# Feed-forward units of a Hymba-style layer: a unit's stores issued one product later, and the splits of the new operands at the turn spread over other products

## The chip, the cores and the metric

The kernel runs on one core of one Trainium2 chip. The metric is the device time of one execution in microseconds (us). Every kernel is run several times, and its time is the median of the runs.

## What is computed

One layer of a bidirectional encoder, in float32, on a sequence of 2048 rows of 1024 values: a modulated RMSNorm, one input projection, windowed attention beside a two-way mLSTM, one output projection with a gated residual, and then a feed-forward part with its own modulated norm and gated residual. The change lies in the feed-forward part alone, which in the reference is

```
h = rms_norm(x, g_norm2) * (1 + scale) + shift        # 2048 x 1024
gu = h @ w_ffn_in                                     # 1024 x 5632
g, u = split(gu, 2)                                   # D_FF = 2816 columns each
x = x + gate * ((silu(g) * u) @ w_ffn_out)            # 2816 x 1024
```

## The kernel before

**A matrix product in three.** TensorE multiplies float32 operands that are split into a high part (`hi`, rounded by a copy on ScalarE) and the rest (`lo`, a subtraction on VectorE). One product of float32 precision is three matmuls, hi by hi, hi by lo and lo by hi (function `mm3`, L56 to L58).

**Seven products for eight.** Both feed-forward matrix products go by a Strassen scheme (Winograd's form): a 2 by 2 block product by seven block products instead of eight. The seven row operands, in the order of use B11, B21, T2, T1, T3, B22 and T4, are sums and differences of blocks of `h`. They lie in DRAM in `hop_d` and are split into resident tiles in SBUF, two tiles of hi and two of lo for each operand. The seven weight operands of a unit (A11, A12, S2, S1, S3, S4, A22) are made from the raw weights by Pool and split by ScalarE and VectorE while the unit before runs (function `weights`, L1455 to L1467).

**A unit.** Function `pair` is one unit: the products 0 to 6, each of 12 matmuls (four times `mm3`), and between them the work on their sums. Three PSUM banks are used, `ps1` for the products 0, 2, 4 and 6, `ps2` for product 1, and `ps5` for products 3 and 5; product after product is added up in the same bank. So a product must wait for the copy of what the bank held before it: product 2 for `s` (L1613, after product 0), product 4 for `u` (L1619), product 5 for `c` (L1624, after product 3), product 6 for `u` (L1627, after product 4). All of these are on ScalarE. There too stands the tanh `t` (L1620), which waits for VectorE's `g` (L1616, the sum of product 1 and `s`), and it stands ahead of `c`. Later in the unit VectorE does `u` (L1631) and `u` (L1633), with the tanh `t` (L1632) on ScalarE between them, and after product 6 L1640. Pool does L1628 and L1639, in the units of one half of the columns L1645, and at the end of each pair of units L1654, L1656 and L1658. The results of a unit go to DRAM (`a_d`); they are put on the list `late`, and the next unit issues their stores on SyncE (function `stores`, L1590).

**The row of units.** There are 44 units: the first 22 on one half of the rows, the other 22 on the other half. The unit in which the first half is used for the last time (number 21, counted from 0) is called the turn. While it runs, the seven operands of the other half are brought in, in the tiles that its products leave: `start(u)` after product `u` loads operand `u` (two DMAs of 512 KB on SyncE, L1412), and `finish(u)` splits it, two copies on ScalarE (L1416) and two subtractions on VectorE (L1417). At the turn `finish` takes operands 0, 1, 2, 3 and 4 after the products 1, 2, 3, 4 and 6; the operands 5 and 6 are split in unit 22, after its products 0 and 1. No weights are prepared during the turn; unit 22 uses weights that are there already, and prepares those of unit 23 from its product 2 on (STEPS).

**What sets the order.** Every engine works through its instructions in the order in which the code writes them. `beside(u)`, called as `then(u)` between two products, writes the splits at the turn and the making of weights into that order. Engines wait for each other by semaphores alone.

The tile names in the rows of the profile are these: `fp` is a PSUM bank of a unit, `B` and `T` are row operands, `A` and `S` are weight operands, and `sf`, `graw` and `A22r` are raw weights and their sums.

Of the kernel before, what the change touches and what calls it, by code (L numbers as in the profile page):

```python
# [36 lines left out]
def hybrid_layer_kernel(  # L37
# [14 lines left out]
    def bank(tag, name):  # L52
        return pp.tile([P, 512], F32, tag=tag, name=name, bufs={"g": 2, "a": 2, "b": 1, "c": 2, "d": 1}[tag])

    def mm3(o, lh, ll, rh, rl, first, last, skip=False):
        pe.matmul(o, lh, rh, start=first, stop=False, skip_group_check=skip)  # L56
        pe.matmul(o, lh, rl, start=False, stop=False, skip_group_check=skip)  # L57
        pe.matmul(o, ll, rh, start=False, stop=last, skip_group_check=skip)  # L58
# [218 lines left out]
    s1 = xs.enter_context(tc.tile_pool(name="sx", bufs=2, side="left", reuse_waits="tile"))  # L277
# [881 lines left out]
    for s_ in range(len(order) + 2):  # L1159
# [22 lines left out]
        u2, u1 = u1, u0  # L1182
# [221 lines left out]
    def refill_ops(hh):  # L1404


        hls = []

        def start(u):
            hls.append([[big(4 * u + 2 * z + i, OPS[u]) for i in range(2)] for z in range(2)])  # L1410
            for i in range(2):
                sp.dma_start(hls[u][1][i].bitcast(F32), hop_d[hh, u, 2 * i:2 * i + 2].rearrange("k p t -> p k t"))  # L1412

        def finish(u):
            for hi, lo in zip(*hls[u]):
                act.activation(hi, lo.bitcast(F32), AF.Copy)  # L1416
                dve.tensor_tensor(lo, lo.bitcast(F32), hi.bitcast(F32), SUB)  # L1417

        return hls, finish, start
# [10 lines left out]
    def load_raw(j):  # L1430

        v = lambda t: t.rearrange("p (k c) -> p k c", c=P)
        g = wp.tile([P, D], F32, tag="wraw", name="graw", bufs=1)
        a21 = wp.tile([P, 512], F32, tag="oth", name="A21", bufs=1)
        cg, cu = (slice(o + j * P, o + (j + 1) * P) for o in (0, DFF))
        sp.dma_start(v(g), w_ffn_in[:, cg].rearrange("(k p) c -> p k c", p=P))
        sp.dma_start(v(a21), w_ffn_in[0:512, cu].rearrange("(k p) c -> p k c", p=P))
        return (g, a21) if "ff" not in pools and j else (g, a21, load_a22(j))
# [8 lines left out]
    def weights(raw, early=False):  # L1447

        g, a21, a22 = raw
        a11, a12 = g[:, :512], g[:, 512:]  # L1450
        ws_ = {}

        def part(n, f):
            t = ws_[n] = ring_tile(n)
            act.activation(t[:, 0, :], f, AF.Copy)  # L1455
            dve.tensor_tensor(t[:, 1, :], f, t[:, 0, :].bitcast(F32), SUB)  # L1456

        f1, f2 = (xd.tile([P, 512], F32, tag="n2", name="sf", bufs=9) if early else
                  pools["ff"].tile([P, 512], F32, tag="sf", name="sf", bufs=2) for _ in range(2))
        pool.tensor_tensor(f1, a21, a22, ADD)  # L1460
        pool.tensor_tensor(f2, f1, a11, SUB)
        part("A11", a11)
        yield True
        part("A12", a12)
        pool.tensor_tensor(a21, a11, a21, SUB)
        yield True
        pool.tensor_tensor(a12, a12, f2, SUB)  # L1467
        part("S2", f2)
        yield True
        part("S1", f1)  # L1470
        yield True
        part("S3", a21)
        yield True
        part("S4", a12)
        yield True
        part("A22", a22)
        yield [ws_[n] for n in ("A11", "A12", "S2", "S1", "S3", "S4", "A22")]
# [6 lines left out]
    for p in range(NPR):  # L1484
# [4 lines left out]
        if p == NPR - 1:  # L1489
            hop, finish_op, refill = refill_ops(0)  # L1490

            def after(u):
                if u == 6:
                    raws.append(load_raw(KH))
                refill(u)
                if u > 2:
                    finish_op(u - 3)
# [79 lines left out]
    with tc.tile_pool(name="ff", bufs=1, side="right", reuse_waits="tile") as ff:  # L1577
        NJ = DFF // P

        def ot(name, shape=(P, 512), dt=F32):  # L1580
            return ff.tile(list(shape), dt, tag="ot", name=name, bufs=6)
# [6 lines left out]
        def stores():  # L1588
            for d, t in late:
                sp.dma_start(d, t)  # L1590
            late.clear()

        def pair(hh, j, ws_, hop, after=lambda u: None, then=lambda u: None):

            def prod(u, ps, first=False):
                w, (hi, lo) = ws_[u], hop[u]
                for k in range(4):
                    ks = slice(k * P, (k + 1) * P)  # L1600
                    mm3(ps, w[:, 0, ks], w[:, 1, ks], hi[k // 2][:, k % 2, :], lo[k // 2][:, k % 2, :],
                        first and k == 0, k == 3, True)
                after(u)

            def store(o, t):
                late.append((a_d[AOP[o], j % KH, :, hh, :], t))

            half = j // KH
            ps1, ps2, ps5 = bank("g", "fp"), bank("c", "fp"), bank("a", "fp")
            prod(0, ps1, True)  # L1610
            stores()
            s1_, g0, t0, u2, c5, u3 = (ot(n) for n in ("s1", "g0", "t0", "u2", "c5", "u3"))
            act.activation(s1_, ps1, AF.Copy)  # L1613
            then(0)
            prod(1, ps2, True)
            dve.tensor_tensor(g0, ps2, s1_, ADD)  # L1616
            then(1)
            prod(2, ps1)
            act.activation(u2, ps1, AF.Copy)  # L1619
            act.activation(t0, g0, AF.Tanh, scale=0.5)  # L1620
            dve.scalar_tensor_tensor(g0, t0, 1.0, g0, ADD, MUL)  # L1621
            then(2)
            prod(3, ps5, True)
            act.activation(c5, ps5, AF.Copy)  # L1624
            then(3)
            prod(4, ps1)
            act.activation(u3, ps1, AF.Copy)  # L1627
            pool.tensor_tensor(c5, c5, u3, ADD)  # L1628
            then(4)
            prod(5, ps5)  # L1630
            dve.tensor_tensor(u2, ps5, u2, ADD)  # L1631
            act.activation(t0, u2, AF.Tanh, scale=0.5)  # L1632
            dve.scalar_tensor_tensor(u2, t0, 1.0, u2, ADD, MUL)  # L1633
            then(5)
            prod(6, ps1)
            a0, a1 = u3, c5
            if not kept:
                a0, a1 = (ff.tile([P, 512], F32, tag=f"ka{i}", name=f"ka{i}", bufs=1) for i in range(2))
            pool.tensor_tensor(a1, c5, u2, MUL)  # L1639
            dve.tensor_tensor(a0, ps1, g0, MUL)  # L1640
            store(("A11", "A12")[half], a0)
            if half:
                store("A22", a1)
            if half == 0:
                pool.tensor_tensor(u2, a0, a1, SUB)  # L1645
                store("S3", u2)
            then(6)
            if not kept:
                kept[half] = a0, a1
                return  # L1650
            kept[half] = a0, a1
            (a11, a21), (a12, a22) = kept[0], kept[1]
            s1_, s2_, s4_ = (a21, a11, u2) if half else (a21, g0, a12)
            pool.tensor_tensor(s1_, a21, a22, ADD)  # L1654
            store("S1", s1_)
            pool.tensor_tensor(s2_, s1_, a11, SUB)  # L1656
            store("S2", s2_)
            pool.tensor_tensor(s4_, a12, s2_, SUB)  # L1658
            store("S4", s4_)
            kept.clear()  # L1660
# [8 lines left out]
        for n, (hh, j) in enumerate(units[:-1]):  # L1669
            ws_, turn = nxt_w, n == NJ - 1  # L1670
            start = lambda u: None
            if turn:
                hop1, finish_op, start = refill_ops(1)
                assert not norms
            STEPS = (0, 0, 1, 1, 2, 2, 1)

            def beside(u):

                nonlocal nxt_w, raw, more_w
                if n == 0 and u in (0, 1, 3):  # L1680
                    finish_op(4 + (u + 1) // 2)
                if n == NJ and u < 2:
                    finish_op(5 + u)
                if turn:
                    if u in (1, 2, 3, 4, 6):
                        finish_op(min(u - 1, 4))
                    if u == 6:
                        raw = load_raw(wseq.popleft())
                    return
                if u == 1:  # L1690
                    more_w = weights(raw)
                for _ in range(STEPS[u]):
                    nxt_w = next(more_w)
                if wseq and u == 6 and n != NJ - 2:
                    raw = load_raw(wseq.popleft())
                if n > 1 and u in (1, 3, 5) and norms and next(norms[0], None) is None:
                    norms.popleft()

            pair(hh, j, ws_, hop, start, beside)
            if turn:  # L1700
                hop = hop1
# [263 lines left out]
```

## Time and profile before

| what | value |
| --- | --- |
| time, median of 3 runs | 2272.53 us (2272.24 to 2273.72) |
| time of the profiled execution | 2272.8 us |
| its span, from the first to the last instruction | 2271.0 us |
| mean granted TensorE clock | 0.995 |
| busy: TensorE | 2222.9 us (98%) |
| busy: VectorE | 1606.1 us (71%) |
| busy: ScalarE | 1060.4 us (47%) |
| busy: Pool | 1065.4 us (47%) |

The profiled execution's time is 1.8 us above its span, and 0.3 us above the median. In the rows of the profile PE is TensorE, DVE VectorE, ACT ScalarE, POOL GpSimd and SP SyncE, whose queue of DMA issues is SPq. A row of the timeline gives start, duration, engine, line, operation, the tiles written and read, their shape and the number of instructions in the row, and in brackets the idle time before it with what ended it. L12 is line 12 of the kernel.

### The profile page before, as it was taken

The page shows a single profiled execution, that of the slowest core. Times are in us where ns is not written, and L with a number is a line of the kernel's source. Part 1 is how long each engine was busy: PE and PEld are TensorE (multiplying, and loading weights), DVE is VectorE, ACT ScalarE, POOL GpSimd, SP SyncE. Part 2 cuts the span into 40 slices and gives each one's busy share as a digit, 9 for nine tenths or more (in the row PEclk, how much of TensorE's full clock was granted, in tenths as well). Part 3 has the DMA queues.
Part 4 walks back from the last instruction along what each step waited for, and adds up shares of the span by engine and source line. Part 5 has one row for each costly group of instructions (what it writes and reads, how often), then busy time and mean ns, then how long its engine had stood idle before and what let it go on. Part 6 is the DMA issues. An engine that isn't in the chain of part 4 may idle for free.

```text
span 2271.0 us, 32441 instructions
## 1 busy us (share of the span) xinstructions
PE 2222.9 (98%) x10822; PEld 1857.2 (82%) x10822; DVE 1606.1 (71%) x2931; ACT 1060.4 (47%) x2206; POOL 1065.4 (47%) x927
## 2 busy tenths in 40 slices
PE   6999999999999999999999999999999999999998
PEld 4997888888888878788888888788888888888886
DVE  6787577656688887786767786766666666785694
ACT  5433655554677746354445444433333333233452
POOL 1006635334344334436666665666566654692020
PEclk9999999999999999999999999999999999999999
DMA  8476755585766575764343454433333374442462
GB/s 331 158 248 213 239 170 165 185 242 173 210 185 181 172 250 197 267 233 149 110 148 112 157 181 165 155 98 111 98 112 98 112 253 145 167 153 94 147 214 93
DMA packets 352811, 391.28 MB, mean 172 GB/s; under 512 B 21260, under 2 KB 251004, under 8 KB 352644
## 3 DMA queue, kind: packets, MB, share of 16 engines
q1 hardware_dynamic: 352420, 389.18, 52.4%
q8 instruction: 85, 1.39, 0.2%
q14 instruction: 82, 0.67, 0.1%
q10 hardware_dynamic: 224, 0.04, 0.0%
HBM read 269.95 MB, written 119.19 MB: 171 GB/s over the span
## 4 chain that ended last, share of the span: by engine, by line
PE 55%; DVE 2%; issue 1%; DMA 0%; ACT 0%; ACTq 0%; DVEq 0%
PE fp L56 12%; PE fp L57 12%; PE fp L58 12%; PE fo L58 6%; PE fo L56 6%; PE fo L57 6%; PE ops L56 1%; PE ops L57 1%; PE ops L58 1%; DMA T<-hop_d 0%; DVE ra L1862 0%; PE trn L183 0%; DVE T L1417 0%; DVE ra L1877 0%; DVE B L1417 0%
## 5 line engine op out<-in xcount | busy, mean ns | idle before, releaser
L498 PE MATMUL gps<-hT,whi 128*128 128x512 f32 x1088 | 395.7, 418 | 0.3 <-DVE cacc L513 0.3
L58 PE MATMUL fo<-w,al 128*128 128x512 f32 x616 | 239.8, 389 | 0.4 <-DVE al L1719 0.4
L57 PE MATMUL fo<-w,ah 128*128 128x512 f32 x616 | 239.7, 389 | 0.0
L56 PE MATMUL fo<-w,ah 128*128 128x512 f32 x616 | 239.7, 389 | 0.0
L498 PE MATMUL gps<-hT,wlo 128*128 128x512 f32 x544 | 226.1, 416 | 0.0
L498 PEld LDWEIGHTS gps<-hT,whi 128*128 128x128 f32 x1088 | 199.5, 190 | 24.2 <-DVE cacc L513 0.7
L56 PE MATMUL fp<-T,S 128*128 128x512 f32 x528 | 206.8, 392 | 0.6 <-ACT s L1613 0.6
L57 PE MATMUL fp<-T,S 128*128 128x512 f32 x528 | 205.7, 389 | 0.0
L58 PE MATMUL fp<-T,S 128*128 128x512 f32 x528 | 205.4, 389 | 0.0
L1719 DVE TENSOR_TENSOR al<-al,ah 128x1024 fp32r<-128x1024 f32 x77 | 116.5, 1518 | 108.4 <-ACT ah L1718 108.2
L1718 ACT ACTIVATE ah<-al 128x1024 fp32r<-128x1024 f32 x77 | 81.6, 1060 | 180.4 <-DMA al<-a_d 178.9
L1456 DVE TENSOR_TENSOR S<-sf,S 128x512 fp32r<-128x512 f32 x86 | 129.9, 1548 | 37.3 <-ACT S L1455 37.1
L1456 DVE TENSOR_TENSOR A<-graw,A 128x512 fp32r<-128x512 f32 x86 | 128.1, 1511 | 14.1 <-ACT A L1455 14.1
L58 PE MATMUL fp<-B,A 128*128 128x512 f32 x352 | 136.9, 389 | 0.0
L56 PE MATMUL fp<-B,A 128*128 128x512 f32 x352 | 136.9, 389 | 0.0
L57 PE MATMUL fp<-B,A 128*128 128x512 f32 x352 | 136.9, 389 | 0.0
L58 PEld LDWEIGHTS fo<-w,al 128*128 128x128 f32 x616 | 115.6, 188 | 24.9 <-DVE al L1719 0.8
L56 PEld LDWEIGHTS fo<-w,ah 128*128 128x128 f32 x616 | 115.7, 188 | 24.1
L57 PEld LDWEIGHTS fo<-w,ah 128*128 128x128 f32 x616 | 115.6, 188 | 23.9
L1621 DVE SCALAR_TENSOR_TENSOR g<-t,g 128x512 f32<-128x512 f32 x44 | 44.3, 1008 | 128.2 <-ACT t L1620 128.2
L798 POOL TENSOR_SCALAR ap<-ap,adn 128x384 f32<-128x384 f32 (+1 forms) x128 | 72.4, 587 | 126.7 <-PE atp L805 58.6
L1460 POOL TENSOR_TENSOR sf<-A,A22r 128x512 f32<-128x512 f32 x43 | 60.8, 1415 | 146.9 <-DMA A22r<-in_w_ffn_in_dram 122.3
(418 smaller groups left out, 6160.3 us busy)
## 6 DMA issues: line engine op xcount, KB each, us to landing
al<-a_d SPq DMA_DIRECT2D x77, 512.0 KB, 3.7
wmod<-in_w_mod_dram SPq DMA_DIRECT2D x48, 512.0 KB, 7.6
graw<-in_w_ffn_in_dram SPq DMA_DIRECT2D x43, 512.0 KB, 3.7
a_d<-ka SPq DMA_DIRECT2D x66, 256.0 KB, 4.6
bc<-bc_d SPq DMA_DIRECT2D x64, 256.0 KB, 3.7
hop_d<-n SPq DMA_DIRECT2D x56, 256.0 KB, 4.4
a_d<-u SPq DMA_DIRECT2D x55, 256.0 KB, 4.6
mqk<-qk_d SPq DMA_DIRECT2D x44, 256.0 KB, 3.9
```

Source lines behind the costliest of these rows:

```text
L56: pe.matmul(o, lh, rh, start=first, stop=False, skip_group_check=skip)
L57: pe.matmul(o, lh, rl, start=False, stop=False, skip_group_check=skip)
L58: pe.matmul(o, ll, rh, start=False, stop=last, skip_group_check=skip)
L498: pe.matmul(ps, w[i == 2][:, k, :], hT[n](i == 1, k), start=(k == 0 and i == 0), stop=(k == KT - 1 and i == 2))
L798: pool.tensor_scalar(self.p[g][:, :self.NK], self.p[g][:, :self.NK], dn[:, g:g + 1], 0.0, MUL, ADD)
L1456: dve.tensor_tensor(t[:, 1, :], f, t[:, 0, :].bitcast(F32), SUB)
L1460: pool.tensor_tensor(f1, a21, a22, ADD)
L1621: dve.scalar_tensor_tensor(g0, t0, 1.0, g0, ADD, MUL)
L1718: act.activation(ah, al.bitcast(F32), AF.Copy)
L1719: dve.tensor_tensor(al, al.bitcast(F32), ah.bitcast(F32), SUB)
```

## The change

Two places of the feed-forward part are edited.

1. The stores of the unit before are issued behind product 1 of a unit instead of behind product 0. The tile for `s` is now taken ahead of them, the other five behind them.
2. At the turn the operands 0 to 5 are split after the products 1 to 6, one each, and only operand 6 is left for unit 22, after its product 0. Before, operand 4 came after product 6, and the operands 5 and 6 after the products 0 and 1 of unit 22.

```diff
@@ pair @@
             prod(0, ps1, True)
-            stores()
-            s1_, g0, t0, u2, c5, u3 = (ot(n) for n in ("s1", "g0", "t0", "u2", "c5", "u3"))
+            s1_ = ot("s1")
             act.activation(s1_, ps1, AF.Copy)
             then(0)
             prod(1, ps2, True)
+            stores()
+            g0, t0, u2, c5, u3 = (ot(n) for n in ("g0", "t0", "u2", "c5", "u3"))
             dve.tensor_tensor(g0, ps2, s1_, ADD)
             then(1)
@@ beside @@
                 if n == 0 and u in (0, 1, 3):
                     finish_op(4 + (u + 1) // 2)
-                if n == NJ and u < 2:
-                    finish_op(5 + u)
+                if n == NJ and u == 0:
+                    finish_op(6)
                 if turn:
-                    if u in (1, 2, 3, 4, 6):
-                        finish_op(min(u - 1, 4))
+                    if u:
+                        finish_op(u - 1)
                     if u == 6:
                         raw = load_raw(wseq.popleft())
                     return
```

After the change `s` is L1612, and from `g` on (L1616 before, L1617 after) the line numbers are one higher. Elsewhere in a unit SyncE has nothing between the two places of the stores, so its row reads the same there, and the rows of TensorE and Pool are the same throughout. Three engines have a new order at the turn.

SyncE at the turn, from the loads of operand 0 on. In these rows a name is followed by its tile's number; B11 is operand 0, B21 operand 1 and T2 operand 2, and the two stores are results of unit 20. Before:

```order
L1412 DMA B11_15310<-hop_d_74 128x2x512
L1412 DMA B11_15311<-hop_d_74 128x2x512
L1590 DMA a_d_76<-ka0_15285 128x512
L1590 DMA a_d_76<-u2_15175 128x512
L1412 DMA B21_15337<-hop_d_74 128x2x512
L1412 DMA B21_15338<-hop_d_74 128x2x512
L1412 DMA T2_15360<-hop_d_74 128x2x512
```

and after:

```order
L1412 DMA B11_15310<-hop_d_74 128x2x512
L1412 DMA B11_15311<-hop_d_74 128x2x512
L1412 DMA B21_15330<-hop_d_74 128x2x512
L1412 DMA B21_15331<-hop_d_74 128x2x512
L1590 DMA a_d_76<-ka0_15285 128x512
L1590 DMA a_d_76<-u2_15188 128x512
L1412 DMA T2_15360<-hop_d_74 128x2x512
```

The loads of operand 1 now stand ahead of the two stores. In the last unit two stores likewise go behind two loads of the second product's weights (`w2x`).

VectorE from the end of the turn (L1633, L1640) into unit 22 (`g`, L1616). T3 is operand 4, B22 operand 5, T4 operand 6. Before:

```order
L1633 SCALAR_TENSOR_TENSOR u2_15319<-t0_15318,u2_15319 128x512
L1640 TENSOR_TENSOR u3_15321<-fp_15293,g0_15317 128x512
L1417 TENSOR_TENSOR T3_15408<-T3_15408,T3_15406 128x1024
L1417 TENSOR_TENSOR T3_15409<-T3_15409,T3_15407 128x1024
L1417 TENSOR_TENSOR B22_15432<-B22_15432,B22_15430 128x1024
L1417 TENSOR_TENSOR B22_15433<-B22_15433,B22_15431 128x1024
L1616 TENSOR_TENSOR g0_15493<-fp_15473,s1_15492 128x512
L1417 TENSOR_TENSOR T4_15453<-T4_15453,T4_15451 128x1024
L1417 TENSOR_TENSOR T4_15454<-T4_15454,T4_15452 128x1024
L1621 SCALAR_TENSOR_TENSOR g0_15493<-t0_15494,g0_15493 128x512
```

and after:

```order
L1634 SCALAR_TENSOR_TENSOR u2_15338<-t0_15337,u2_15338 128x512
L1417 TENSOR_TENSOR T3_15408<-T3_15408,T3_15406 128x1024
L1417 TENSOR_TENSOR T3_15409<-T3_15409,T3_15407 128x1024
L1641 TENSOR_TENSOR u3_15340<-fp_15293,g0_15336 128x512
L1417 TENSOR_TENSOR B22_15432<-B22_15432,B22_15430 128x1024
L1417 TENSOR_TENSOR B22_15433<-B22_15433,B22_15431 128x1024
L1417 TENSOR_TENSOR T4_15457<-T4_15457,T4_15455 128x1024
L1417 TENSOR_TENSOR T4_15458<-T4_15458,T4_15456 128x1024
L1617 TENSOR_TENSOR g0_15514<-fp_15477,s1_15491 128x512
L1622 SCALAR_TENSOR_TENSOR g0_15514<-t0_15515,g0_15514 128x512
```

Operand 4's pair has gone ahead of L1640, and operand 6's pair ahead of `g`: six splits now stand between L1633 and `g`, where there were four.

ScalarE in the same place, with `s` (L1613) of unit 22. Before:

```order
L1632 ACTIVATE t0_15318<-u2_15319 128x512
L1416 ACTIVATE T3_15406<-T3_15408 128x1024
L1416 ACTIVATE T3_15407<-T3_15409 128x1024
L1613 ACTIVATE s1_15492<-fp_15472 128x512
L1416 ACTIVATE B22_15430<-B22_15432 128x1024
L1416 ACTIVATE B22_15431<-B22_15433 128x1024
L1416 ACTIVATE T4_15451<-T4_15453 128x1024
L1416 ACTIVATE T4_15452<-T4_15454 128x1024
L1619 ACTIVATE u2_15495<-fp_15472 128x512
L1620 ACTIVATE t0_15494<-g0_15493 128x512
L1455 ACTIVATE A11_15539<-graw_15463 128x512
L1624 ACTIVATE c5_15496<-fp_15474 128x512
```

and after:

```order
L1633 ACTIVATE t0_15337<-u2_15338 128x512
L1416 ACTIVATE T3_15406<-T3_15408 128x1024
L1416 ACTIVATE T3_15407<-T3_15409 128x1024
L1416 ACTIVATE B22_15430<-B22_15432 128x1024
L1416 ACTIVATE B22_15431<-B22_15433 128x1024
L1612 ACTIVATE s1_15491<-fp_15476 128x512
L1416 ACTIVATE T4_15455<-T4_15457 128x1024
L1416 ACTIVATE T4_15456<-T4_15458 128x1024
L1620 ACTIVATE u2_15516<-fp_15476 128x512
L1621 ACTIVATE t0_15515<-g0_15514 128x512
L1455 ACTIVATE A11_15539<-graw_15467 128x512
L1625 ACTIVATE c5_15517<-fp_15478 128x512
```

The two copies of operand 5 have gone ahead of `s`; the rest stands as it stood.

## The prediction

> **What bounds the kernel now.** I read the page's busy line first, then busy time by windows around the turn, then TensorE's waits there, and last the timelines of the engines that end them.
>
> ```profile
> PE 2222.9 (98%) x10822; PEld 1857.2 (82%) x10822; DVE 1606.1 (71%) x2931; ACT 1060.4 (47%) x2206; POOL 1065.4 (47%) x927
> ```
>
> TensorE is the bound: it is busy 98% of the span. A change elsewhere counts only where TensorE waits.
>
> ```profile
> 1300.00:1400.00 100.00, 100.00 (x451) 1.00 0.44 150
> 1400.00:1425.00 25.00, 23.80 (x105) 1.00 0.86 307
> 1425.00:1450.00 25.00, 23.36 (x103) 1.00 0.31 104
> PE fp L56 <- ACT c L1624: 2.2, 2, 1.2
> PE fp L56 <- ACT s L1613: 0.6, 1, 0.6
> PE fo L58 <- DVE al L1719: 0.4, 1, 0.4
> ```
>
> The first three rows are windows: length, TensorE's busy time, its clock (1.00 is full), DMA share, GB/s. The units before the turn leave no gap. The turn and unit 22 leave 1.20 + 1.64 = 2.84 us. The waits from 1400 to 1475 us are three (fourth and fifth row: total, times, longest). From 1450 us to the end there is only the last row, 0.4 us, in the second product of the feed-forward part. So the stores that move in the other units, and in the last one, move beside a full TensorE and are worth nothing, and **a gain is at most 2.85 us, 0.13%**. What a measurement of this kernel can tell from no change is about 0.2%, 4.5 us; by that the change can hardly show as faster. It can show as slower.
>
> Here are the three waits in the timeline, with a pair of rows for a product's length:
>
> ```profile
> 1406.57 0.39 PE L56 MATMUL fp<-T,S 128*128 128x512 f32 x1
> 1409.29 0.39 PE L56 MATMUL fp<-T,S 128*128 128x512 f32 x1
> 1416.10 0.50 PE L56 MATMUL fp<-B,S 128*128 128x512 f32 x1 [1.21 <-ACT c L1624]
> 1436.46 0.50 PE L56 MATMUL fp<-B,S 128*128 128x512 f32 x1 [1.03 <-ACT c L1624]
> 1448.27 0.50 PE L56 MATMUL fp<-T,S 128*128 128x512 f32 x1 [0.61 <-ACT s L1613]
> ```
>
> Two products in a row start 2.72 us apart; a unit is seven, 19.04 us. The waits are ahead of product 5 of the turn, product 5 of unit 22 and product 2 of unit 23.
>
> **The stores at the turn (first edit).**
>
> ```profile
> 1402.46 1.73 SPq L1412 DMA_DIRECT2D B<-hop_d  x2
> 1405.32 0.33 SPq L1590 DMA_DIRECT2D a_d<-ka  x1
> 1407.08 0.33 SPq L1590 DMA_DIRECT2D a_d<-u  x1
> 1407.51 0.93 SPq L1412 DMA_DIRECT2D B<-hop_d  x2
> 1405.44 1.62 POOL L1645 TENSOR_TENSOR u<-ka,ka 128x512 f32<-128x512 f32 x1 [1.29 <-DVE ka L1640]
> 1413.21 1.06 ACT L1416 ACTIVATE B<-B 128x1024 fp32r<-128x1024 f32 x1 [2.60 <-DMA B<-hop_d]
> 1414.50 1.06 ACT L1416 ACTIVATE B<-B 128x1024 fp32r<-128x1024 f32 x1 [0.23 <-DMA B<-hop_d]
> 1415.46 0.58 ACT L1624 ACTIVATE c<-fp 128x512 f32<-128x512 f32 x1
> ```
>
> The loads of operand 1 stand at 1407.51 behind the store of `u`, which waits for Pool's L1645 (to 1407.06). ScalarE copies them as they land, and `c` behind the second copy ends too late for product 5: that is the 1.21 us. Now those loads pass both stores. They have to wait for their tiles alone, which product 1 reads last before 1406.57, so they go one to two microseconds earlier and land that much earlier; the two stores and operand 2 go later, and the copies of operand 2 stand behind `c`. I take the 1.21 us as gone. What is late next is `u` (L1627) ahead of product 6, which stands behind operand 2's copies: between 0 and 1.2 us, taken as 0.4, because the window 1400 to 1425 shows the DMA engines at 0.86 of their time, so that later loads gain little from the order. The tile for `s` is now taken ahead of the stores, so `s` of unit 23 waits for a store that was issued in unit 22, six products or 16 us before; that costs nothing.
>
> **The splits (second edit).** This is the term that decides.
>
> ```profile
> 1424.77 0.68 DVE L1640 TENSOR_TENSOR u<-fp,g 128x512 f32<-128x512 f32 x1
> 1425.37 4.25 DVE L1417 TENSOR_TENSOR T<-T,T 128x1024 fp32r<-128x1024 f32 x2
> 1429.54 4.54 DVE L1417 TENSOR_TENSOR B<-B,B 128x1024 fp32r<-128x1024 f32 x2
> 1434.00 0.68 DVE L1616 TENSOR_TENSOR g<-fp,s 128x512 f32<-128x512 f32 x1
> 1434.60 3.94 DVE L1417 TENSOR_TENSOR T<-T,T 128x1024 fp32r<-128x1024 f32 x2
> 1434.78 0.63 ACT L1620 ACTIVATE t<-g 128x512 f32<-128x512 f32 x1 [4.00 <-DVE g L1616]
> 1435.31 0.61 ACT L1455 ACTIVATE A<-graw 128x512 fp32r<-128x512 f32 x1
> 1435.83 0.58 ACT L1624 ACTIVATE c<-fp 128x512 f32<-128x512 f32 x1
> ```
>
> L1640 started at 1424.77 right behind L1633, and VectorE has no idle time from there on. Before, `g` started 1434.00 − 1424.77 = 9.23 us behind the end of L1633: L1640 and four splits. Behind `g` ScalarE's `t`, a weight copy and `c` follow, and product 5 started at 1436.46, 2.46 us after `g` did. Now six splits and L1640 stand ahead of `g`. By the starts of these rows that is 4.17 + 0.60 + 4.46 + 3.86 = 13.09 us (the last is 3.94 less the 0.08 by which the first pair's row runs into the next), and product 5 can start 13.09 + 2.46 = 15.55 us behind the end of L1633, where it was 11.69: **3.86 us later**. How early L1633 ends depends on the loads at the turn; with those of operand 1 earlier it is 0 to 0.8 us earlier, and I take 0.6. That leaves 3.2 us, between 3.0 and 3.9.
>
> How long TensorE waits there shows on ScalarE:
>
> ```profile
> 1425.92 0.58 ACT L1613 ACTIVATE s<-fp 128x512 f32<-128x512 f32 x1
> 1426.40 2.00 ACT L1416 ACTIVATE B<-B 128x1024 fp32r<-128x1024 f32 x2
> ```
>
> Before, `s` was followed by the two copies of operand 5, which ended at 1426.40 + 2.00 = 1428.40. Now they change places with it, and `s` ends there, 3.6 us behind the end of L1633. Product 2 waits for it; it was at 1416.10 + 4 × 2.72 = 1426.98, and with the 1.21 us gone it would be ready before that, so a wait of about 1.5 us (0.7 to 1.5) is new here. Product 5 is wanted three products later, 3.6 + 8.16 = 11.8 us behind L1633, and can go at 15.55: **one wait of 3.8 us (3.6 to 4.2)** where 1.03 us was. The 0.61 us in unit 23 go, since everything behind has 3 us more of TensorE's lateness to be ready in; if not, the sum grows by that.
>
> So the waits add 3.2 − 0.6 = **+2.6 us** (1.5 to 3.5: the lower end with L1633 earlier still and splits at the lower mean, the upper with loads no earlier). Counted the other way, 0.4 + 1.5 + 3.8 = 5.7 against 2.85 gives +2.85.
>
> **The clock.** A wait of 3.8 us is longer than any that the feed-forward part has now, and another part of the trace shows what such a wait can bring:
>
> ```profile
> 819.94:823.35 3.41, 1.57 (x8) 1.00 1.07 381
> 823.35:826.77 3.42, 2.14 (x9) 0.50 0.91 301
> 826.77:830.18 3.41, 3.41 (x10) 0.50 0.03 11
> 830.18:833.59 3.41, 3.41 (x17) 1.00 0.15 39
> 1413.86:1417.27 3.41, 2.21 (x10) 1.00 1.05 405
> 1434.34:1437.75 3.41, 2.38 (x11) 1.00 0.06 22
> 826.72 0.63 PE L58 MATMUL ops<-wo,mS 128*128 128x512 f32 x1
> 827.14 0.63 PE L56 MATMUL ops<-wo,mS 128*128 128x512 f32 x1
> ```
>
> In steps of 3.41 us, the window in which TensorE was busy 1.57 us is followed by a granted clock of 0.50, until a full window has passed. The windows busy 2.21 and 2.38 us, around two of our waits, have no such sequel. Behind the drop two matmuls stand 0.42 us apart, where 2.72 / 12 = 0.227 is usual: 47% of the time at half clock is lost. A wait of 3.8 us lies over two windows at the least, and one of them then holds 1.9 us of it or more and is busy 1.5 us or less; that is the drop's side of these rows. The half clock then lasts one full window of work, 0.47 × 3.41 = 1.6 us, or the rest of one and another, up to 2.8 us. I take **+2.2 us**, the middle.
>
> By the Trainium skill ("TensorE: Matmul & The Clock Gate", section "What's actually happening") the clock is halved after at least one idle window of about 3.4 us, and the windows run free. By that rule a wait of 3.8 us would have to hold a whole window, which only (3.8 − 3.4) / 3.4, 12% of the phases, would do; the sum would be without the 2.2 us. The window at 819.94 was idle 1.84 us of 3.41 and was followed by half clock all the same, so I go by the trace.
>
> **The sum.** 2272.8 + 2.6 + 2.2 = 2277.6 us for the profiled execution, which stood 0.3 us above the median of the runs: **2277.3 us**, +0.21%.
>
> **The rivals.**
>
> *The clock stays.* The mechanism: half a window idle is not enough, and what fell at 819.94 fell for something else beside. For it speak the two windows at the turn without a drop; against it the 1.57 row, whose neighbour the new wait would be. The waits alone: 2272.5 + 2.6 = 2275.1 us (2274.0 to 2276.0). Chance 0.20.
>
> *The loads land late as well.* Two stores and operand 2 now share the DMA engines with operand 1's tail, at a share of 1.05 from 1413.86 on. If L1633 ends no earlier and a split more is held up, the wait is 4.2 us and the waits add 3.5; the idle time then lies so that nearly two windows run at half clock, 2.8 us. 2272.5 + 6.3 = 2278.8 us. Chance 0.14.
>
> *VectorE gets through the splits in time: not slower.* The splits of the run took 3.86 to 4.46 us a pair. A split without Pool beside it is much shorter, as the row before shows:
>
> ```profile
> 1414.30 2.51 DVE L1417 TENSOR_TENSOR B<-B,B 128x1024 fp32r<-128x1024 f32 x2 [2.84 <-ACT B L1416]
> 1430.85 2.15 POOL L1658 TENSOR_TENSOR u<-u,ka 128x512 f32<-128x512 f32 x1
> ```
>
> 1.25 us each there, and 2.1 in the rows above, with Pool at work at the same time (the second row, 2.15 us for one operation, is one of several in a row). Pool's L1656 now waits for L1640, which stands behind a pair, so the two engines are shifted against each other. The wait of 3.8 us is gone when the six splits average 1.5 us instead of 2.08. Then the clock stays too, and of the 2.85 us about 1.9 (0.4 and 1.5) come back: −1.0, 2271.5 us; with those gone too 2269.7. Against it: Pool has seven operations in a row there, and they fill the time of six splits. Chance 0.06.
>
> **How the numbers follow.** The forecast has 0.60, with a range of its own from 2276.5 to 2278.3 us. A slower result by over 0.2% is one over 2277.1: some 0.44 of the forecast's 0.60 and all 0.14 of the late loads, 0.58. The rest of the forecast (0.16), the case with a steady clock (0.20) and most of the fast splits (0.04) lie within 0.2%: 0.40. Faster by over 0.2%, under 2268.0, is left 0.02. The range reaches from 2273.6, below the waits without a clock drop, to 2278.9.
>
> **What would show it right or wrong.** Right: in the changed kernel's waits the 1.21 us ahead of product 5 of the turn is gone, a wait for `s` of about 1.5 us stands ahead of product 2 of unit 22 and one for `c` of about 3.8 us ahead of its product 5, VectorE runs six splits and L1640 for 13 us without idle time ahead of `g`, and the granted clock is 0.50 in one or two windows behind. A clock of 1.00 there gives the first rival; splits of 1.5 us or less give the last. It is all wrong if units away from the turn show new waits of TensorE.

## The result and the profile after

The changed kernel takes 2276.36 us (median of 22 runs, 2272.95 to 2284.51), the kernel before 2272.20 us (median of 22 runs, 2269.29 to 2277.01). The ratio is 1.0021, with a 95% interval from 1.0015 to 1.0026: slower by 0.21% (the two medians alone are 0.18% apart). The profiled execution took 2277.64 us with a span of 2275.9 us, 4.9 us longer than before.

Busy time by windows (length, TensorE's busy time, clock, DMA share, GB/s) and TensorE's waits from 1400 to 1475 us of the changed kernel:

```profile
1400.00:1425.00 25.00, 25.00 (x111) 1.00 0.79 282
1425.00:1450.00 25.00, 19.73 (x79) 0.93 0.37 128
1450.00:1475.00 25.00, 25.00 (x112) 1.00 0.31 95
PE fp L56 <- ACT c L1625: 4.0, 1, 4.0
PE fp L56 <- ACT s L1612: 1.3, 1, 1.3
```

The turn itself is without a gap now. In its place 1425 to 1450 us has lost 5.27 us, where both windows together had lost 2.84 us, and its clock is 0.93. Two waits are left of three, both in unit 22, and both are where the prediction put them.

Not all of the 4.9 us is the change. TensorE's timeline gives the start of the turn and of unit 24, three units later, for the kernel before (first two rows) and the changed one:

```profile
1401.13 0.39 PE L56 MATMUL fp<-B,A 128*128 128x512 f32 x1
1462.00 0.39 PE L56 MATMUL fp<-B,A 128*128 128x512 f32 x1
```

```profile
1402.78 0.39 PE L56 MATMUL fp<-B,A 128*128 128x512 f32 x1
1467.42 0.39 PE L56 MATMUL fp<-B,A 128*128 128x512 f32 x1
```

That stretch took 60.87 us before and 64.64 us after: **+3.8 us**. The turn began 1.65 us later for reasons ahead of it, where the two kernels do the same, and what follows unit 24 took 0.5 us less. Over all the profiles of this study the turn begins between 1397.6 and 1402.8 us, so that spans of single executions can't be compared to a microsecond; the stretch can, and it is used below. (57.1 us of it are work: three units of 19.04 us.)

The two waits in TensorE's timeline, and VectorE's and ScalarE's part in them:

```profile
1428.75 0.50 PE L56 MATMUL fp<-T,S 128*128 128x512 f32 x1 [1.29 <-ACT s L1612]
1441.18 0.50 PE L56 MATMUL fp<-B,S 128*128 128x512 f32 x1 [3.97 <-ACT c L1625]
1424.46 0.69 DVE L1634 SCALAR_TENSOR_TENSOR u<-t,u 128x512 f32<-128x512 f32 x1 [0.76 <-ACT t L1633]
1425.41 4.46 DVE L1417 TENSOR_TENSOR T<-T,T 128x1024 fp32r<-128x1024 f32 x2 [0.26 <-ACT T L1416]
1429.80 0.68 DVE L1641 TENSOR_TENSOR u<-fp,g 128x512 f32<-128x512 f32 x1
1430.40 3.95 DVE L1417 TENSOR_TENSOR B<-B,B 128x1024 fp32r<-128x1024 f32 x2
1434.27 4.53 DVE L1417 TENSOR_TENSOR T<-T,T 128x1024 fp32r<-128x1024 f32 x2
1438.72 0.68 DVE L1617 TENSOR_TENSOR g<-fp,s 128x512 f32<-128x512 f32 x1
1428.12 0.58 ACT L1612 ACTIVATE s<-fp 128x512 f32<-128x512 f32 x1
1439.49 0.63 ACT L1621 ACTIVATE t<-g 128x512 f32<-128x512 f32 x1 [7.09 <-DVE g L1617]
1440.55 0.58 ACT L1625 ACTIVATE c<-fp 128x512 f32<-128x512 f32 x1
```

`g` starts 13.57 us behind the end of L1634 (1425.15), with six splits and L1641 ahead of it; ScalarE stands 7.09 us at `t`, and `c`, behind `t`, lets product 5 go at 1441.18. `s` ends behind the copies of operand 5 and holds product 2. Behind the long wait the clock falls, as windows of its steps of 3.41 us show:

```profile
1435.13:1438.54 3.41, 2.07 (x10) 1.00 0.00 0
1438.54:1441.96 3.42, 0.78 (x3) 1.00 0.00 0
1441.96:1445.37 3.41, 3.41 (x9) 0.50 0.00 0
1445.37:1448.78 3.41, 3.41 (x16) 1.00 0.00 0
```

One window at half clock costs 0.47 × 3.41 = 1.6 us. Waits of 5.26 us instead of 2.85 and 1.6 us of half clock make +4.0 us, against the 3.8 us of the stretch. (Two waits stand in it where there were three; what a wait costs beside its bracket is said under the table below.)

### The profile page after: what moved, and what is told of

Read it like the earlier page. It is cut to its first block, busy times and chain, and to the rows that moved or that the text cites. A ratio compares the mean times of both kernels' runs of the same rounds, so it can differ in the third digit from the quotient of the medians.

```text
span 2275.9 us, 32442 instructions
## 1 busy us (share of the span) xinstructions
PE 2224.1 (98%) x10822; PEld 1858.3 (82%) x10822; DVE 1608.3 (71%) x2931; ACT 1060.4 (47%) x2206; POOL 1067.2 (47%) x927
## 4 chain that ended last, share of the span: by engine, by line
PE 56%; DVE 1%; issue 1%; DMA 1%; ACT 0%; POOL 0%; ACTq 0%; DVEq 0%; POOLq 0%
PE fp L56 12%; PE fp L57 12%; PE fp L58 12%; PE fo L57 6%; PE fo L56 6%; PE fo L58 6%; PE ops L56 1%; PE ops L57 1%; PE ops L58 1%; DMA T<-hop_d 1%; PE trn L183 0%; DVE T L1417 0%; DVE S L1456 0%; DVE B L1417 0%; POOL sf L1461 0%
## 5 line engine op out<-in xcount | busy, mean ns | idle before, releaser
L1456 DVE TENSOR_TENSOR S<-sf,S 128x512 fp32r<-128x512 f32 x86 | 131.3, 1565 | 34.8 <-ACT S L1455 34.5
L1456 DVE TENSOR_TENSOR A<-graw,A 128x512 fp32r<-128x512 f32 x86 | 127.9, 1508 | 15.5 <-ACT A L1455 15.4
```

## The experiments

The theory: the slowdown is VectorE's six splits ahead of `g`, which make one wait of 4 us, and a half clock that this wait sets off. The rivals: the stores' new place has part in it; the copies of operand 5 ahead of `s` are what counts; the half clock is an accident or costs nothing; the splits are long of themselves and not because of Pool. The table gives for each kernel the waits of TensorE from the turn to unit 23 (sum of its timeline's brackets), the stretch from the turn to unit 24 against 60.87 us before, the time at half clock in it, and the ratio to the kernel before on the same chip.

| kernel | waits, us | stretch, us | against before | half clock, us | ratio, 95% interval |
| --- | --- | --- | --- | --- | --- |
| before | 2.85 | 60.87 | | 0 | |
| the change | 5.26 | 64.64 | +3.8 | 3.41 | 1.0021 (1.0015 to 1.0026) |
| change_again | 5.75 | 66.47 | +5.6 | 6.83 | 1.0027 (1.0016 to 1.0038) |
| stores_alone | 2.44 | 60.48 | −0.4 | 0 | 0.9996 (0.9987 to 1.0005) |
| splits_alone | 6.53 | 66.14 | +5.3 | 3.41 | 1.0019 (1.0010 to 1.0028) |
| op6_behind_g | 1.77 | 59.90 | −1.0 | 0 | 0.9998 (0.9989 to 1.0007) |
| wait_filled | 2.38 and 3.2 of filling | 63.59 | +2.7 | 0 | 1.0011 (1.0002 to 1.0020) |
| pool_to_vector | 2.87 | 60.95 | +0.1 | 0 | 1.0003 (0.9994 to 1.0011) |
| g_first | 1.73 | 59.78 | −1.1 | 0 | 0.9997 (0.9988 to 1.0006) |
| g_first_vector | 1.25 | 58.98 | −1.9 | 0 | 0.9993 (0.9984 to 1.0001) |
| g_first_vector_again | 0.95 | 58.72 | −2.1 | 0 | 0.9993 (0.9984 to 1.0001) |
| copies_later | 0.61 | 58.05 | −2.8 | 0 | 0.9993 (0.9984 to 1.0002) |

In every row the difference from before is explained by the waits and 0.47 of the working time at half clock, to 0.6 us or better. Most of what is left over goes with the number of waits. Beside the 57.1 us of work, the brackets and the clock, 0.32 us remain in copies_later with its one wait, 0.66 us in the change with two and 0.90 us in the kernel before with three: in these kernels a wait costs about 0.3 us more than its bracket shows.

### Each part alone

Only the stores are moved:

```diff
-                if n == NJ and u == 0:
-                    finish_op(6)
+                if n == NJ and u < 2:
+                    finish_op(5 + u)
                 if turn:
-                    if u:
-                        finish_op(u - 1)
+                    if u in (1, 2, 3, 4, 6):
+                        finish_op(min(u - 1, 4))
```

> Only the stores go behind product 1; the splits stand as before the change. My theory: the 1.21 us ahead of product 5 of the turn goes, because operand 1's loads pass the stores, but VectorE's run of splits behind L1634 starts no earlier, so product 5 of unit 22 starts where it did (1436.5 us, give or take 0.5) and the wait ahead of it grows from 1.0 to about 2.3 us; time within 0.7 us of before, clock at 1.00. The other reading, that the stores' move is a gain of its own: waits of 1.6 us in all and 1.2 us off the time. The third, that the stores' move is part of what made the change slower: waits over 3.5 us.

TensorE's waits of this kernel:

```profile
PE fp L56 <- ACT c L1625: 1.1, 1, 1.1
PE fp L56 <- ACT u L1628: 0.7, 1, 0.7
PE fp L56 <- ACT s L1612: 0.6, 1, 0.6
```

The wait ahead of product 5 of the turn is gone, and 0.7 us ahead of product 6 stands in its place, as the prediction's term for the stores said. What I expected further is a miss: the wait ahead of product 5 of unit 22 did not grow to 2.3 us but stayed at 1.1, because VectorE came out of the turn 0.4 us earlier too, not at the same time as before. The stores' move gains 0.4 us of the stretch; in the time that doesn't show. It is no part of the slowdown. (The stretch is one execution's: the two profiles of g_first_vector, the same kernel, differ by 0.3 us.)

Only the splits are moved (the second hunk of the change, on the kernel before):

> Only the order of the splits is new; the stores are where they were. My theory: VectorE has the same six splits and L1640 ahead of g, so a wait of 3.5 to 4.0 us stands ahead of product 5 of unit 22, with the 1.2 us at the turn still there; waits of 5.3 to 6.5 us in all, and 0.50 of the clock for one or two windows behind: 4 to 6 us over before. If the stores' move was part of the slowdown: a wait below 2.5 us, no drop of the clock, and less than 2 us over before.

```profile
PE fp L56 <- ACT c L1624: 5.4, 2, 4.0
PE fp L56 <- ACT s L1613: 1.1, 1, 1.1
1436.17:1439.58 3.41, 0.58 (x3) 1.00 0.00 0
1439.58:1442.99 3.41, 3.41 (x10) 0.50 0.00 0
```

The same wait of 4.0 us and the same half clock, with the 1.4 us at the turn besides. The slowdown is the splits' alone.

### Which of the moved splits

In the changed kernel operand 6 goes back behind `g`:

```diff
-                if n == NJ and u == 0:
+                if n == NJ and u == 1:
                     finish_op(6)
```

> The whole change, but operand 6 is split after product 1 of unit 22 as before the change, so only four splits and L1641 stand ahead of g. My theory: g starts some 9.3 us behind the end of L1634 instead of 13.6, c is there when product 5 wants it (wait 0 to 0.4 us), the wait for s of 1.3 us ahead of product 2 stays, the clock stays at 1.00; within 1 us of before, and 3 to 5 us below the change. If what counts is the copies of operand 5 ahead of s, or the amount of splitting in the turn, the time stays within 1.5 us of the change.

```profile
PE fp L56 <- ACT s L1612: 1.8, 2, 1.3
```

With this pair of splits behind `g` the wait for `c` is gone altogether, the 1.3 us ahead of product 2 stay, 0.5 us for `s` in unit 23 stand beside them, and the half clock is gone. So one pair of splits on the wrong side of one instruction is the whole loss; the copies ahead of `s` and operand 4's pair ahead of L1641 cost nothing on balance.

### The clock apart from the wait

In the changed kernel TensorE gets work that nothing reads, in the place where it waits:

```diff
             then(4)
+            if fill:                       # 14 in unit 22
+                spare = bank("b", "spare")
+                w, (hi, lo) = ws_[0], hop[0]
+                for i in range(fill):
+                    pe.matmul(spare, w[:, 0, :P], hi[0][:, 0, :], start=True, stop=True, skip_group_check=True)
             prod(5, ps5)
```

> The whole change, and 14 matmuls more on TensorE between products 4 and 5 of unit 22, into a bank that nothing reads: 14 x 0.227 = 3.2 us of the 4.0 us that TensorE waits there anyway. My theory, that the slowdown is a wait of its own and a drop of the clock on top: product 5 starts at the same place, the clock stays at 1.00, and the time is 1.6 us (1.2 to 2.8) below the change and 2 to 3 us above before. If the half clock came from something other than TensorE's idleness, or costs nothing: the time is that of the change or above it, and 0.50 still shows.

The filling and product 5 in the timeline, and the window around them:

```profile
1433.83 3.33 PE L1635 MATMUL spare<-B,A 128*128 128x512 f32 x14
1437.97 0.50 PE L56 MATMUL fp<-B,S 128*128 128x512 f32 x1 [0.80 <-ACT c L1625]
1434.91:1438.33 3.42, 2.62 (x12) 1.00 0.00 0
```

Product 5 is as late as in the change, 3.17 + 0.80 us, but the clock stays at 1.00 throughout. The stretch is 63.59 us, which is the waits and the filling alone (5.55 − 2.85 = +2.7), 1.1 and 2.9 us below the two profiles of the change: 14 useless matmuls make this stretch shorter. The ratio of the times is the lower one too, but the intervals overlap, so that the times alone don't show it. The half clock is set off by TensorE's idleness in that wait, and it has a price of its own.

The changed kernel once more:

> The changed kernel once more, for a second look at the clock at another place of its steps of 3.41 us. My theory: the waits are 5.0 to 6.0 us in all again, with 3.8 to 4.1 us ahead of product 5 of unit 22, and one or two windows at 0.50 follow; the stretch from the turn to unit 24 is 3 to 5 us longer than before. If the half clock of the first look was an accident: 1.00 throughout, and the stretch 2.2 to 2.8 us longer than before.

```profile
1437.39:1440.80 3.41, 0.41 (x2) 1.00 0.00 0
1440.80:1444.21 3.41, 2.43 (x6) 0.50 0.00 0
1444.21:1447.62 3.41, 3.41 (x10) 0.50 0.00 0
1447.62:1451.04 3.42, 3.42 (x17) 1.00 0.00 0
```

The wait is 3.97 us again, but lies otherwise against the windows: the first window at half clock still holds the end of the wait, and a second one follows. That is 2.43 + 3.41 = 5.84 us of work at half clock, 0.47 × 5.84 = 2.7 us. With them the stretch is 5.6 us longer than before, outside the 3 to 5 us that I expected. The clock's price is 1.6 us in two profiles (the change, splits_alone) and 2.7 us in one.

### Pool beside the splits

In the changed kernel Pool's work beside the splits is done by VectorE:

```diff
 # weights, for unit 23 (eng = dve)
-        pool.tensor_tensor(f1, a21, a22, ADD)
-        pool.tensor_tensor(f2, f1, a11, SUB)
+        (eng or pool).tensor_tensor(f1, a21, a22, ADD)
+        (eng or pool).tensor_tensor(f2, f1, a11, SUB)
 # pair, at the turn (eng = dve)
-            pool.tensor_tensor(s1_, a21, a22, ADD)
+            eng.tensor_tensor(s1_, a21, a22, ADD)
 ...           # s2_ and s4_ likewise
```

> The whole change, with Pool's work beside the six splits given to VectorE: L1655, L1657 and L1659 of the turn and the two sums of raw weights L1460 and L1461 of unit 22. My theory, that Pool makes the splits long: they take 1.25 us each instead of 2.1, and although VectorE does three operations of 0.7 us more ahead of g, g starts 10 to 11 us behind the end of L1634 instead of 13.6; the wait ahead of product 5 of unit 22 falls from 4.0 to 1.0 to 1.7 us, the clock stays at 1.00, the time is 3 to 4.5 us below the change and within 1 us of before. If the splits are long for a reason of their own: 2.1 us each still, g 15 us or more behind L1634, a wait of 5 us or more, and a time above the change.

VectorE's timeline from L1634 to `g`:

```profile
1422.32 0.69 DVE L1634 SCALAR_TENSOR_TENSOR u<-t,u 128x512 f32<-128x512 f32 x1 [0.76 <-ACT t L1633]
1423.27 3.39 DVE L1417 TENSOR_TENSOR T<-T,T 128x1024 fp32r<-128x1024 f32 x2 [0.26 <-ACT T L1416]
1426.59 0.68 DVE L1641 TENSOR_TENSOR u<-fp,g 128x512 f32<-128x512 f32 x1
1427.19 2.34 DVE L1417 TENSOR_TENSOR B<-B,B 128x1024 fp32r<-128x1024 f32 x2
...
1431.50 2.35 DVE L1417 TENSOR_TENSOR T<-T,T 128x1024 fp32r<-128x1024 f32 x2
1433.77 0.68 DVE L1617 TENSOR_TENSOR g<-fp,s 128x512 f32<-128x512 f32 x1
```

Without Pool a pair takes 2.34 us, where it took 3.95 to 4.53 us; only the first, beside Pool's L1640 (1423.15 to 1424.44), takes 3.39. `g` starts 1433.77 − 1423.01 = 10.8 us behind the end of L1634, although VectorE does three operations more ahead of it, and the wait for `c` is 1.09 us. The prediction's third rival is thus a true mechanism: with 1.35 us a split on average the wait of 4 us shrinks and the clock stays. It did not come about in the change because Pool was not out of the way. Its price of −1.0 us was not measured, since VectorE here has Pool's operations to do as well (stretch +0.1 us). The Trainium skill ("SBUF — State Buffer", section "SBUF: two separate sides") calls the pair of ports that GpSimd shares with VectorE, there where an operation of VectorE has two inputs in SBUF as a split has, an exclusive lock, whose loser waits for the whole of the other's instruction; the doubling of the splits beside Pool, and its end without Pool, agree, and so does the first pair: it ran beside L1640 for 1.17 us and took 1.05 us longer than a pair without Pool.

### Versions with `g` first

```diff
-                if n == NJ and u == 0:
-                    finish_op(6)
+                if n == NJ and u == 1:
+                    finish_op(5)
+                    finish_op(6)
                 if turn:
-                    if u:
-                        finish_op(u - 1)
+                    if u in (1, 2, 3, 4, 6):
+                        finish_op(min(u - 1, 4))
```

> The stores as the change has them, the splits in another order: operand 4 after product 6 of the turn as before the change, and the operands 5 and 6 both after product 1 of unit 22, behind g; s ahead of the copies of operand 5. My theory: g and c are never late, but the splits of the operands 5 and 6 themselves are, since VectorE with Pool beside it needs 2.1 us for each: waits of 0.5 to 1 us ahead of product 5 and 1 to 1.5 us ahead of product 6 of unit 22; the time within 1 us of before, clock at 1.00. If only the place of g counts, the waits fall below 1 us in all and the time is 2 us below before.

```profile
PE fp L56 <- ACT s L1612: 0.9, 1, 0.9
PE fp L58 <- DVE A L1456: 0.8, 1, 0.8
```

A miss in the place: the splits of operands 5 and 6 are in time, and what is late instead are the weights of unit 23 (`A`, L1456) that VectorE splits behind them, and `s` of unit 23. The sum, 1.7 us, lies in the 1.5 to 2.5 us that I expected.

With pool_to_vector's edit as well:

> The order of g_first and the work of pool_to_vector on VectorE together. My theory: with splits of 1.25 us the operands 5 and 6 are there in time, TensorE waits 0.3 to 1 us in all from the turn to unit 23 where it waited 2.85 us, and the time is 1.8 to 2.6 us below before, the lowest of all. If VectorE's added operations delay g, or the weights of unit 23, as much as the splits gain: waits of 2 us or more, time within 0.8 us of before.

> g_first_vector once more, for a narrower interval: 1.3 us of waits from the turn to unit 23 again, the stretch within 0.3 us of 137.9, and a time 1.2 to 2.4 us below before. If the first look was an accident of the loads: a stretch of 138.5 us or more.

Waits of 1.25 and 0.95 us (0.3 to 1 us was expected first), and a stretch 1.9 and 2.1 us shorter than before. The 137.9 us of this expectation and the next are counted over another, longer length, which is not given; by the table the second profile's stretch is 0.3 us shorter than the first's. Last, operand 2 is split after product 4 of the turn instead of product 3:

> As g_first_vector, but operand 2 is split after product 4 of the turn, with operand 3, so that ScalarE's u (L1628) no longer stands behind its copies. My theory: the wait of 0.68 us ahead of product 6 of the turn goes and nothing takes its place, 0.6 us for s in unit 23 stays; the stretch from the turn to unit 24 is 0.4 to 0.8 us shorter than in g_first_vector (137.9 us), the time 2.0 to 3.2 us below before. If VectorE's split of operand 2 is what the end of the turn hangs on: L1632 goes later by about 1 us, a wait stands in unit 22, and the stretch stays at 137.9 us or grows.

```profile
PE fp L56 <- ACT s L1612: 0.6, 1, 0.6
```

One wait of 0.6 us is left, and the stretch is 58.05 us, 0.9 us above the bare work and 0.7 and 0.9 us below the two profiles of g_first_vector. The time is a miss: 1.3 us below before by the medians, where 2.0 to 3.2 was expected. The times of these versions are the lowest of all, 2269.1 to 2269.8 us, and clearly below the change. Against the kernel before they are at 0.9993 three times, each time with an interval that reaches 1: what the stretch shows, some 2 to 3 us, is hardly more than the half width of these intervals (0.0009, 2.0 us), so that a gain in the time is not shown.

## Why the prediction was right

The time was 2276.36 us where 2277.3 was forecast, inside the range of 2273.6 to 2278.9 and just under the forecast's own of 2276.5 to 2278.3, and the step from before 4.2 us (medians) where 4.8 was forecast. That the ratio of 1.0021 is the forecast's +0.21% to the last digit is luck; the mechanism is not. Its steps, one by one:

- **The stores.** Right. The 1.21 us ahead of product 5 of the turn went, and 0 to 0.7 us ahead of product 6 came in the kernels with this edit (0.4 taken): none in the first profile of the change, 0.48 us in the second. Elsewhere no wait can be put down to the edit. A wait of 0.60 us for `s` at 1019.29 in the first units of the changed kernel (0.29 us in change_again, none in the kernel before) stands ahead of the first store that was moved, which SyncE issued at 1022.44. From unit 24 to the end the changed kernel has no wait; change_again has one of 1.0 us in the second product and the kernel before one of 0.4 us.
- **The wait for `s`.** 1.29 us by its bracket, where about 1.5 was said (0.7 to 1.5). The prediction counted from start to start, and so it is 1.49 us (1428.75 − 1416.38 − 4 × 2.72).
- **The wait for `c`.** 3.97 us by its bracket, where 3.8 was said (3.6 to 4.2); from start to start, as the prediction counted, 4.27 us (1441.18 − 1428.75 − 3 × 2.72), a little above that range. For the place of product 5, two terms were off and partly made up for each other. L1634 ended 22.4 us after the start of the turn (1425.15 − 1402.78), where it had been 23.6 us (1424.77 − 1401.13): 1.3 us earlier, outside the 0 to 0.8 that I allowed. I had taken operand 1 alone to be earlier, but operand 2 was earlier too (below): VectorE began its pair at 14.47 us (1417.25 − 1402.78) instead of 15.90 (1417.03 − 1401.13). And the run ahead of `g` took 13.6 us instead of 13.1: VectorE stood 0.26 us for ScalarE's copy, which I had excluded, and the three pairs took 4.46, 3.95 and 4.53 us, 12.94 in all, where the rows of before added up to 12.73. Product 5 came 38.40 us after the start of the turn instead of 35.33, 3.1 us later; 3.2 was said.
- **Unit 23.** Its 0.61 us went, as said.
- **The sum of the waits.** By the brackets +2.4 us in the first profile and +2.9 in the second, where +2.6 was said. By the starts it is +2.1 us in the first, 3.07 less the 0.93 us by which product 2 of unit 23 is no longer late (1448.27 − 1436.46 − 4 × 2.72).
- **The clock.** It fell each of the three times that the wait of 4 us stood, and stayed in the stretches of the nine other profiles. The price of 1.6, 1.6 and 2.7 us brackets the 2.2 us taken.

One reading of the prediction was wrong, and it goes with L1634's early end: operand 2's loads do not go later. SyncE issued the first of them here, before (first row) and in the change:

```profile
1408.53 6.53 SPq L1412 DMA_DIRECT2D T<-hop_d  x6
1409.63 7.08 SPq L1412 DMA_DIRECT2D T<-hop_d  x6
```

Counted from the start of the turn that is 7.40 us (1408.53 − 1401.13) before and 6.85 us (1409.63 − 1402.78) in the change. Before, SyncE stood at the store of `u` with operand 1's loads behind it; now those go ahead of the store.

The first rival, in which the clock stays, is refuted by the windows, and wait_filled shows what it would have looked like: 1.0011 (1.0002 to 1.0020) instead of 1.0021 (1.0015 to 1.0026). By the Trainium skill ("TensorE: Matmul & The Clock Gate", section "What's actually happening") half clock follows a window of about 3.4 us that was idle; here windows that were busy 0.41, 0.58 and 0.78 us of 3.41 were followed by it, so the rule as stated would have given the wrong case. The second rival, loads so late that the wait grows to 4.2 us, did not come about, though its price for the clock did once. The third is settled above.

## What to carry to other kernels

Before a piece of side work is moved, look for the first instruction behind its new place that the bound engine waits for, and add up what now stands ahead of that instruction on its engine: here one pair of splits, 4.5 us, ahead of one addition was the whole loss, and the same pair behind it costs nothing. Price such side work by rows in which the neighbour engine is as busy as it will be there, not by its duration alone. A wait that leaves TensorE busy for less than about half of a 3.41 us window costs more than its length; the waits of 1.4 us and less in these stretches didn't reach that, and filling a long one with useless matmuls can pay, as the stretch of wait_filled shows.

## What the runs showed of the hardware

The half clock is decided by how much of a window is busy, as far as these windows show, and the bound looks sharp. Here are windows of this study in the output projection at about 820 us, where matmuls 512 wide run with a few of one column between them, from three kernels in the order op6_behind_g (three rows), pool_to_vector and splits_alone (two rows each):

```profile
819.66:823.08 3.42, 1.63 (x7) 1.00 1.10 379
823.08:826.49 3.41, 1.56 (x8) 1.00 1.01 337
826.49:829.90 3.41, 3.41 (x9) 0.50 0.05 20
```

```profile
821.54:824.95 3.41, 1.62 (x10) 1.00 1.10 373
824.95:828.36 3.41, 3.41 (x10) 0.50 0.34 129
```

```profile
818.35:821.77 3.42, 2.20 (x10) 1.00 1.09 382
821.77:825.18 3.41, 2.57 (x13) 1.00 0.97 323
```

Busy 1.63 and 2.20 us: the clock stayed. Busy 1.62 and 1.56 us: 0.50 in the next window. The other profiles agree from 80 us to the last matmul: every window at full clock that was busy 1.62 us or less was followed by half clock, and none that was busy 1.63 us or more (the nearest are 1.65 us in g_first_vector_again from 2255.24 and 1.69 us in the change from 168.78). So it lies near 1.6 us of 3.41, 47 to 48% as the profile counts busy time, and a wait of 3.97 us can't be shared out over two windows without one of them falling below. It does not hold for all matmuls: in the kernel before, a window among matmuls 272 wide was busy 2.60 us and was followed by half clock all the same,

```profile
51.94:55.36 3.42, 2.60 (x12) 1.00 0.80 259
55.36:58.77 3.41, 3.41 (x12) 0.50 0.94 373
```

and why is left open. The windows lie otherwise against the program in each execution, as the two profiles of the change show. So the kernels, which are the same up to the place at 820 us, meet it differently: splits_alone and wait_filled have no window at half clock there, the kernel before and the change have two, change_again has one. That may be one source of the spread between runs of the same kernel; it was not measured by itself.
